# Moving the sample group's attention into the merge stage of a hybrid decoder step, with evacuations ranked first and a pipelined final stage

## Chip, cores, metric

One Trainium2 chip, all 8 cores (two dies of four). Each core runs the same program on one prompt sequence of 2048 tokens and on 16 of the 128 sample tokens. The metric is the device time of the slowest core, in microseconds. Runs come fast and slow (one die at a lower granted clock). Ratios are of fast runs. Medians are of all runs of a kernel; where one of these was slow (before, a_nosample, a_a2, the first session of the changed kernel), the median of its fast runs alone is at most 0.7 us lower.

## The reference, cut to what matters

```python
u = rmsnorm(x, norm_g); proj = u @ w_in                    # 1024 -> 8704 columns
lx, lg, sb, scg, sh, sg, q, qg, mg = split(proj)
xc = causal_dwconv(lx) + b; hs = rglru(xc)                 # A: gates, decay, scan over time
z_a = (hs * silu(lg)) @ lru_wo
z_b = (silu(sg) * sb * causal_dwconv(scg * sh)) @ sconv_wo # B
z_c = (softmax(q k / sqrt(128)) v * silu(qg)) @ xa_wo      # C: 256 memory tokens, 4 heads
g_a, g_b, g_c = split(sigmoid(mg))
y = x + (g_a*z_a + g_b*z_b + g_c*z_c) @ w_out              # then a final rmsnorm
```

The prompt group shares one set of keys and values per core. In the sample group each of the 16 tokens has its own 256 keys and values, so its attention is 16 small problems, each with a 512 KB key tile and a 512 KB value tile to fetch.

## The kernel before

The kernel is written as a graph of tasks with a rank (`prio`, smaller is earlier). At build time a planner with its own idea of durations fixes one order per engine; on the chip every engine follows its order strictly. So a changed rank is a changed order, and nothing on the chip corrects a bad one. Two words used below: a *unit* is the group of matmuls that fills one PSUM tile (16 for a projection), and its *evacuation* is the ScalarE or VectorE operation that reads that tile and so frees it for the next unit.

```python
PS = Ring("psum", ..., 4)                  # four PSUM tiles of 128 x 1024 fp32
def branch_A_lx(n, P):                     # one projection, three units of 688 columns
    for u, ps in enumerate(proj(C_LX + n * 128, P)):
        G.act(copy(lxp[u] <- ps), ..., P - 20 + u)         # evacuation: rank P - 20
    ...                                    # convolution on ScalarE and VectorE, rank P + 2
def branch_A_gates(n, P):                  # six gate units of 2 matmuls, tanh on ScalarE,
    ...                                    # then exp, exp, sqrt, multiply, scan
# planner: a task whose table set is not loaded counts as 20 later
for n in range(NCH + 1):                   # "block n": six channel blocks of 128
    branch_B_sb(n - 1); branch_A_gates(n); attend(n)       # attend only for n < 4
    branch_A_lg(n + 1)
    if n == 3:
        sample_scores(pos, 5.0)            # 16 x (broadcast matmul, multiply, reduce)
        sample_values(pos + 90, 1.5)       # 16 x 8 matmuls of one column
    branch_B_c(n - 1); branch_B_sg(n + 1); branch_A_lx(n + 1)
# merge stage: 8 column blocks, each: gate projection, tanh, output matmuls, multiply-add
# final stage: 17 row tiles
for ti in range(17):
    ps = mT @ wo                                            # 16 matmuls of 512 columns
    y = 0.5 * ps + x                                        # VectorE, line 1138
    stat = sum(y * y)                                       # ScalarE, line 1141
    rstd                                                    # GpSimd, lines 619, 621
    y = y * stat * fgb                                      # VectorE, line 1145
    store y   # writes t_dram[4], so each store waits for the last one
```

The softmax here doesn't subtract the row's maximum and nothing guards it: scores larger than these inputs give would overflow.

## Time and profile before

| what | value |
|---|---|
| first session, timed | 876.95 us median of 4 (873.47 to 881.83) |
| later session, timed | 859.72 us median of 8 (one of them slow) |
| profiled span, slowest core | 858.4 us |
| blocks (116.6 to 487.2 us) | 370.6 us, 82 more than TensorE's work takes at full pace |
| merge (487.2 to 771.2) | 284.0 us, TensorE busy 283.1 |
| final (771.2 to 858.4) | 87.2 us, against 58.8 of matmuls |

How to read it: TensorE does most of the work, so time is either TensorE's own or time in which it waits. The share of the chain that ended last says how much is left to win. Part 4 of the page gives that chain by engine:

```profile
PE 64%; ACT 9%; DVE 9%; issue 9%; DMA 4%; POOL 3%; ACTq 1%; DVEq 0%; POOLq 0%; SPq 0%
```

64% of the span lay on TensorE, and 36% on other engines, on transfers and on issue. For the final stage the view of waits on VectorE (what waited, what for: total us, times, longest) names the two reasons:

```profile
DVE R L1145 <- POOL R L621: 27.2, 13, 2.5
DVE R L1138 <- DMA y_p<-R: 6.5, 1, 6.5
```

VectorE stood 27.2 us for the norm from GpSimd (13 tiles, 2.5 us each at most), in order, so the next residual and with it the next PSUM tile waited too.

### The profile page before, as it was taken

The numbers are of one execution on the slowest core, as the hardware profiler recorded it, in microseconds if no ns is written. First come the engines' busy times: TensorE is split into PE (matmuls) and PEld (weight loads), VectorE is DVE, ScalarE is ACT, GpSimd is POOL, SyncE is SP. The second block draws the span as 40 slices with busy tenths as digits, with TensorE's granted clock in tenths as the row PEclk, the third lists the DMA queues.
The fourth block names the chain that finished last, engine by engine and source line by source line (L and its number), as shares of the span: only waits on it lengthen the run. The fifth ranks groups of instructions, "written<-read, shape, count | busy, mean of one in ns | idle before, by whom it ended". The sixth has DMA issues, their size and how long they took to land.

```text
span 858.4 us, 13185 instructions; the slowest of 8 cores (848.3 to 858.4 us)
## 1 busy us (share of the span) xinstructions
PE 742.9 (87%) x4859; PEld 460.8 (54%) x4859; DVE 386.3 (45%) x367; ACT 339.1 (40%) x398; POOL 251.2 (29%) x301
## 2 busy tenths in 40 slices
PE   0699989789888977979896699999999999999880
PEld 0466546356445544536554466666666666664330
DVE  0432244637636636798978161222222122224364
ACT  2355378784684484446354122112122221212221
POOL 2875200202002111101224234436344352232121
PEclk9999999889989989989998899999999999999996
DMA  6897962223223325556265559343443340019632
GB/s 133 215 181 108 147 98 26 24 26 38 25 39 36 37 26 87 119 122 135 44 85 70 74 62 125 32 40 35 40 42 38 34 40 2 1 26 316 237 136 101
DMA packets 109449, 68.67 MB, mean 80 GB/s; under 512 B 90819, under 2 KB 97045, under 8 KB 109371
## 3 DMA queue, kind: packets, MB, share of 16 engines
q0 software_dynamic: 96640, 30.81, 34.4%
q1 hardware_dynamic: 12508, 36.69, 13.3%
q8 instruction: 40, 0.66, 0.3%
q10 hardware_dynamic: 239, 0.34, 0.2%
q14 instruction: 22, 0.18, 0.1%
HBM read 88.96 MB, written 9.82 MB: 115 GB/s over the span
## 4 chain that ended last, share of the span: by engine, by line
PE 64%; ACT 9%; DVE 9%; issue 9%; DMA 4%; POOL 3%; ACTq 1%; DVEq 0%; POOLq 0%; SPq 0%
PE PP L726 61%; DVE R L804 2%; ACT R L1141 2%; DMA y_p<-R 2%; DVE R L1138 2%; ACT R L790 2%; DVE R L777 1%; POOL R L621 1%; DMA R<-sconv_w 1%; DVE R L803 1%; ACT R L939 1%; DMA R<-cv 1%; PE PP L866 1%; DVE R L838 1%; POOL R L633 1%
## 5 line engine op out<-in xcount | busy, mean ns | idle before, releaser
L726 PE MATMUL PP<-R 128*128 128x344 bf16 x4104 | 632.0, 315 | 34.4 <-ACT R L790 7.7
L726 PEld LDWEIGHTS PP<-R 128*128 128x128 bf16 x4104 | 402.1, 99 | 256.9 <-issue 55.4
L1101 DVE SCALAR_TENSOR_TENSOR R<-R,PP 128x688 f32<-128x688 f32 x72 | 62.7, 871 | 202.8 <-PE PP L726 202.7
L131 POOL DMA_DIRECT2D R<-w_in x68 | 60.4, 889 | 307.0 <-PE PP L726 270.3
L1095 ACT ACTIVATE R<-PP 128x688 f32<-128x688 f32 x72 | 53.6, 744 | 218.4 <-PE PP L726 218.4
L1134 PE MATMUL PP<-R 128*128 128x512 bf16 (+1 forms) x272 | 60.0, 379 | 8.4 <-DVE R L1138 7.3
L1105 POOL TENSOR_TENSOR R<-R 128x688 f32<-128x688 f32 x24 | 39.3, 1639 | 45.6 <-DVE R L1101 44.1
L1134 PEld LDWEIGHTS PP<-R 128*128 128x128 bf16 (+1 forms) x272 | 25.9, 97 | 42.3 <-issue 11.9
L1141 ACT ACTIVATE R<-R 128x1024 f32<-128x1024 f32 (+1 forms) x17 | 18.0, 1056 | 65.9 <-DVE R L1138 65.7
L1108 POOL TENSOR_TENSOR R<-R 128x688 bf16<-128x688 f32 x24 | 38.7, 1637 | 16.9 <-DVE R L1101 16.9
L777 DVE SCALAR_TENSOR_TENSOR R<-R 128x2048 f32<-128x2048 f32 x18 | 42.2, 2347 | 2.7 <-ACT R L774 1.9
L642 DVE TENSOR_TENSOR R<-PP,R 128x1024 bf16<-128x1024 bf16 (+1 forms) x19 | 22.1, 1175 | 43.6 <-PE PP L639 43.6
L1145 DVE SCALAR_TENSOR_TENSOR R<-R 128x1024 f32<-128x1024 f32 (+1 forms) x17 | 21.8, 1283 | 28.6 <-POOL R L621 27.2
L619 POOL TENSOR_SCALAR R<-R 128x1 f32<-128x1 f32 (+1 forms) x36 | 8.7, 242 | 87.8 <-ACT R L1141 63.3
L838 DVE SCALAR_TENSOR_TENSOR R<-R 128x2048 f32<-128x2048 f32 x12 | 28.2, 2348 | 8.8 <-ACT R L835 8.4
L790 ACT ACTIVATE R<-PP,R 128x688 f32<-128x688 f32 x36 | 28.1, 833 | 6.8 <-PE PP L726 6.7
L1138 DVE SCALAR_TENSOR_TENSOR R<-PP,R 128x1024 f32<-128x1024 f32 (+1 forms) x17 | 20.5, 1218 | 14.5 <-DMA y_p<-R 6.5
L804 DVE TENSOR_TENSOR_SCAN R<-R 128x2048 f32<-128x2048 f32 x6 | 26.5, 4422 | 0.4
L639 PE MATMUL PP<-R 128*128 128x128 bf16 (+1 forms) x152 | 14.0, 248 | 14.4 <-POOL R L633 13.0
L771 ACT COPY R<-PP 128x688 f32<-128x688 f32 x18 | 13.2, 732 | 29.9 <-PE PP L726 29.9
L829 ACT COPY R<-PP 128x688 f32<-128x688 f32 x18 | 13.0, 730 | 28.8 <-PE PP L726 26.1
L835 ACT ACTIVATE R<-R 128x2048 f32<-128x2048 f32 x6 | 12.0, 1999 | 30.9 <-DVE R L769 18.1
(121 smaller groups left out, 571.3 us busy)
## 6 DMA issues: line engine op xcount, KB each, us to landing
R<-w_in POOLq DMA_DIRECT2D x68, 256.0 KB, 4.6
R<-xp SPq DMA_DIRECT2D x32, 512.0 KB, 7.5
R<-ck SPq DMA_DIRECT2D x16, 512.0 KB, 4.3
y_p<-R SPq DMA_DIRECT2D x16, 512.0 KB, 2.7
R<-cv POOLq DMA_DIRECT2D x16, 256.0 KB, 7.4
R<-w_out POOLq DMA_DIRECT2D x8, 256.0 KB, 7.4
R<-lru_wo POOLq DMA_DIRECT2D x8, 192.0 KB, 3.9
R<-sconv_wo POOLq DMA_DIRECT2D x8, 192.0 KB, 4.1
```

Of the source, the lines that this page charges most:

```text
L131: eng.dma_start(out=out, in_=in_).then_inc(sems[semkey], 16)
L726: return lambda e: e.matmul(ps.ap[:, b * 512:b * 512 + BLK], lhs(k), rhs[:, k, c:c + BLK], start=(k == 0), stop=(k == nk - 1))
L777: G.dve(lambda e, k=k: e.scalar_tensor_tensor(out=xc[:, 0:T], in0=lxp[:, k:k + T], scalar=cw(k), in1=xc[:, 0:T], op0=ALU.mult, op1=ALU.add ...
L790: G.act(lambda e, ps=ps, dst=dst, u=u, bcol=bcol: e.activation(out=cols(dst, u), in_=pv(ps), func=AF.Tanh, scale=0.5, bias=dv[:, bcol:bcol ...
L804: G.dve(lambda e: e.tensor_tensor_scan(out=xc[:, 0:T], data0=thr[:, 0:T], data1=thi[:, 0:T], initial=0.0, op0=ALU.mult, op1=ALU.add), T, t ...
L838: G.dve(lambda e, k=k: e.scalar_tensor_tensor(out=cy[:, 0:T], in0=cinp[:, k:k + T], scalar=sw(k), in1=cy[:, 0:T], op0=ALU.mult, op1=ALU.ad ...
L1095: G.act(lambda e, ps=pg[u], th_=th_: e.activation(out=b3(th_.ap), in_=pv(ps), func=AF.Tanh, scale=0.5), UW, [pg[u].tok], [th_.tok], Px - 2 ...
L1101: G.dve(lambda e, zp=zp, th_=th_, dst=dst: e.scalar_tensor_tensor(out=b3(dst.ap), in0=b3(th_.ap), scalar=1.0, in1=pv(zp), op0=ALU.add, op1 ...
L1105: G.pool(lambda e, acc=acc, th_=th_: e.tensor_tensor(out=acc.ap, in0=acc.ap, in1=th_.ap, op=ALU.add), 1.6, [acc.tok, th_.tok], [acc.tok], Px)
L1108: G.pool(lambda e, acc=acc, th_=th_, u=u, j=j: e.tensor_tensor(out=mT[:, j, u * UW:(u + 1) * UW], in0=acc.ap, in1=th_.ap, op=ALU.add), 1.6 ...
L1134: return lambda e: e.matmul(ps.ap[0:nr, b * 512:(b + 1) * 512], mT[:, k, c0:c0 + nr], wo[:, k, b * 512:(b + 1) * 512], start=(k == 0), sto ...
L1138: G.dve(lambda e, ps=ps, y_=y_, x_=x_, nr=nr: e.scalar_tensor_tensor(out=y_.ap[0:nr, :], in0=ps.ap[0:nr, :], scalar=0.5, in1=x_.ap[0:nr, : ...
```

## The change

Intent: take the sample attention out of the blocks, where VectorE is short, and put it where VectorE idles; keep PSUM flowing by ranking evacuations first; let the final stage run at TensorE's pace.

```diff
+EV = 100
+AB = 20
-  [ps.tok], [t_lx[u]], P - 20 + u          # and so for every evacuation
+  [ps.tok], [t_lx[u]], P - EV + u
-  ... [t_xcP], P + 2)                      # branch A chain
+  ... [t_xcP], P + 2 - AB)
-  k += 20.0                                # table set not loaded
+  k += 40.0 if t.tset else 15.0            # 15: a matmul whose reader needs another set
-  m_a2 = Mem("a2", m_lxp.off, TT, F32)     # decay term over the convolution input
+  m_a2 = side("a2", 0, TT, F32)
-  NW = 12                                  # weight buffers; early loads get a second ring
+  NW = 10
 # sample attention: from block 3 to the merge, its buffers over those of w_out
-  if n == 3: sample_scores(pos, 5.0); sample_values(pos + 90, 1.5)
+  if j == 0: sample_scores(P, 5.0)
+  if j == 3: sample_values(P - 20, 1.0)
+  # column blocks 0 to 4 are merged before the sample columns are ready: keep their tanh and
+  # sum in thS, acS and redo those 16 columns after block 5
+  if j == NJS: fix_samples(P + 6)
 # final stage
-  for xi, x in enumerate((0, 1, 2)):
+  for xi, x in enumerate((0, 1, 2) if j < 7 else (2, 1, 0)):   # frees C's and B's memory early
+  x_ = Handle(xaring if ti % 10 < 4 else xgring)               # one ring for each
+  if last is not None: G.after(last, res)   # scale of tile t behind residual of t + 1
-  store(..., [y_.tok], [t_dram[4]])
+  store(..., [y_.tok], [])
... (cuts: the planner's durations, buffer offsets, one V ring rule)
```

## The prediction

> **What bounds the kernel now.** I read the profile in this order: the page's slices, a table of busy time by stretch that I cut at the first gate matmul of each of the six channel blocks, TensorE's waits, then the timeline at three places. The slices first; the last line is the clock granted to TensorE in tenths:
>
> ```profile
> PE   0699989789888977979896699999999999999880
> DVE  0432244637636636798978161222222122224364
> PEclk9999999889989989989998899999999999999996
> ```
>
> One slice is 858.4/40 = 21.5 us. From slice 23 to 36 TensorE is at 9 and at full clock: the merge stage, which no evacuation order can shorten. The losses lie before it (sevens, sixes and a lowered clock) and after it (eights). VectorE is at 7 to 9 in slices 16 to 20 only. The stretches:
>
> ```profile
> 167.40:233.60 66.20, 59.54 (x369) 36.13 (x370) 37.23 (x32) 42.12 (x45) 9.42 (x13) 0.93 0.29 29
> 233.60:301.90 68.30, 59.47 (x372) 36.12 (x373) 37.39 (x32) 43.05 (x46) 9.41 (x13) 0.95 0.30 35
> 301.90:379.30 77.40, 63.79 (x371) 36.33 (x371) 51.16 (x44) 39.47 (x41) 10.84 (x15) 0.91 0.47 79
> 379.30:441.50 62.20, 57.93 (x358) 34.78 (x359) 56.39 (x45) 31.41 (x29) 11.71 (x16) 0.95 0.49 93
> 441.50:487.20 45.70, 30.75 (x288) 19.58 (x287) 25.02 (x25) 20.09 (x20) 16.58 (x18) 0.85 0.66 92
> 487.20:771.20 284.00, 283.13 (x1947) 189.95 (x1944) 73.29 (x81) 54.56 (x72) 111.80 (x95) 1.00 0.36 39
> 771.20:858.40 87.20, 59.99 (x272) 25.87 (x272) 41.38 (x35) 19.53 (x34) 17.23 (x36) 0.90 0.56 197
> ```
>
> Columns: stretch, length, busy us (and count) of PE, PEld, DVE, ACT, POOL, then granted clock, DMA share, GB/s. The merge row gives a yardstick: 1936 matmuls of 344 columns by the program's order in 283 us, so 0.146 us each. A 512-column one costs 0.216 us (the final stage's 3.46 us for 16). By these, blocks 0 to 5 (116.6 to 487.2 us, 370.6 us long) hold 40.3, 55.1, 56.0, 57.8, 53.0 and 26.3 us of TensorE work: a full block is 348 matmuls x 0.146 = 50.8, plus its attention matmuls, plus 0.36 for each broadcast of the sample scores (6.5 us over 407 ns mean, with 16 of them). What is lost is 10.5, 11.1, 12.3, 19.6, 9.2 and 19.4 us: **82 us**. The two long ones hold the sample attention:
>
> ```profile
> PE PP L1003 <- DMA R<-cv: 13.7, 2, 6.9
> PE PP L726 <- ACT R L790: 7.7, 14, 1.4
> PE PP L964 <- DVE R L832: 4.8, 1, 4.8
> ```
>
> TensorE stood twice for 6.8 and 6.9 us for a value tile (buffers reused at once in a ring of two), and 4.8 us because VectorE was full. Each such pause costs again afterwards:
>
> ```profile
> 340.96 0.58 PE L964 MATMUL PP<-R 16*128 16x512 bf16 x1 [4.76 <-DVE R L832]
> 341.74 7.33 PE L726 MATMUL PP<-R 128*128 128x344 bf16 x32 [0.20 <-DVE R L832]
> 349.01 0.39 PE L964 MATMUL PP<-R 16*128 16x512 bf16 x1
> 349.33 4.84 PE L726 MATMUL PP<-R 128*128 128x344 bf16 x32
> ```
>
> The same 32 matmuls take 7.33 us after the pause and 4.84 us once warm: 2.5 us more.
>
> In the final stage, VectorE is the in-order engine that ties a loop:
>
> ```profile
> 813.10 3.61 PE L1134 MATMUL PP<-R 128*128 128x512 bf16 x16 [1.32 <-DVE R L1138]
> 814.75 0.55 POOL L621 TENSOR_TENSOR R<-R 128x1 f32<-128x1 f32 x1
> 815.47 1.28 DVE L1145 SCALAR_TENSOR_TENSOR R<-R 128x1024 f32<-128x1024 f32 x1 [2.52 <-POOL R L621]
> 816.67 2.35 DVE L1138 SCALAR_TENSOR_TENSOR R<-PP,R 128x1024 f32<-128x1024 f32 x2
> ```
>
> It adds the residual (L1138), idles 2.52 us while ScalarE and GpSimd make the norm, scales (L1145), and only then frees the next PSUM tile. So a tile costs 4.93 us (811.73 to 816.67) and TensorE needs 3.46. Earlier in that stage VectorE waits 6.5 us for a store, since each store waits for the last one, and the first stores run behind twelve 512 KB reloads issued at 770.4.
>
> **What the Trainium skill says.** "TensorE: Matmul & The Clock Gate", Part 1 (the HAM clock gate): after about 3.4 us of idleness the array runs at half clock until about 3.4 us of work have passed. The trace agrees: 7.33 against 4.84 us above, after 4.76 us. "Perfetto Trace Analysis", Optimization Strategy: where the contended engine changes with the regime, interleave the regimes. That is the move here: VectorE is 91% busy in block 4 (56.4 of 62.2 us) and 26% in the merge (73.3 of 284). "ScalarE: Activation LUTs", What ACT_TABLE_LOAD costs: about 1283 ns for the load. The trace shows 1283 ns each, 32 of them in the program. "DMA: Bandwidth & Descriptors", Issuing engines are not separate DMA queues: all transfers share 16 engines. The trace agrees in the first store, 15.8 us behind the reloads on the chain that ended last.
>
> **The change part by part.** I also compared the two programs' instruction orders, which the diff does not give.
>
> 1. *Sample attention goes to the merge.* Out of blocks 3 to 5 go 16 x (1.22 + 1.22) = 39 us of VectorE work, 16 key and most value loads, and 9.4 us of TensorE work (16 x 0.36, 128 small matmuls of 0.025, transposes). That TensorE work comes back in the merge, so it nets zero. The gain is the waits: 13.7 us for values and some 4 us of cold clock after them, and about 9 us of excess in block 3 over block 2.
>
> 2. *Evacuations first, chain of branch A 20 earlier, a buffer of its own for the decay term (before it lay over the convolution's input).* The build's order shows what this does: the gates of block n+1 used to come about five units after the last convolution input, and now come after six branch-B and six further units, some 28 us of TensorE work against the 11 us (scaling 2.1, three times 2.35, cast 1.9) that the convolution needs. ScalarE's order holds 32 table loads before and after, so nothing is saved there. What stays is the burst of six gate units (6 x 0.83 = 5 us of ScalarE for 1.75 us of matmuls) and attention (about 9 us of ScalarE for 5.2 us of matmuls). For 0 to 5 I estimate losses of 8, 7, 7, 7, 4 and 3 us, so 36 in place of 82. This is the softest step. Parts 1 and 2 together: **-46 us**.
>
> 3. *The merge pays.* Fix-up: 20 small matmuls, two tiny VectorE operations, ten small copies and tanhs, all beside TensorE work but for about 1 us. Scores: a key buffer turns round in 4.3 us landing plus 1.2 us of multiplying, so two give one per 2.8 us, against 16 scores spread over some 400 matmuls (59 us, 3.7 us apart). VectorE will stand for a key now and then, and with it the evacuations behind; the four PSUM tiles hide most. I put 4 us. Values: eight buffers for sixteen tiles. Four tiles are consumed, then two units (4.7 us) follow, and then a tile is wanted whose buffer has just come free and takes 7.4 us to land plus about 0.9 to issue: a wait of some 3.5 us, and another for the last four. With a little cold clock, 9 us. Sum **+14 us**, and 10 us of moved work besides.
>
> 4. *Final stage.* The scale of tile t is forced behind the residual of t+1, so VectorE needs 2.5 us a tile and the norm (2.9 us) hides in TensorE's 3.46. Stores no longer wait for one another. Ten reloads start when the last column block has read branch C and then B, some 12 to 25 us before the stage. So 17 x 3.46 = 58.8, plus 0.3, plus the last tile's tail, 7.7 us as now (850.7 to 858.4): 66.8 in place of 87.2, **-20 us**.
>
> Sum: -46 + 14 - 20 = -52, so a span of 806 us. The timed runs of before stand at 879.9 against a profiled span of 858.4, a ratio of 1.025 whose cause the profile doesn't tell; applied to 806 it gives **826**. I take 824.
>
> **Rivals.** *(a) TensorE is fed all through:* blocks then lose some 15 us and the merge almost nothing. Span about 775, timed 795. For it: ScalarE has only about 43 of 68 us to do in a block, VectorE 37. Against it: both are in order, a scan takes 4.4 us at a stretch and a burst of gates outruns ScalarE whatever the ranks. *(b) The waits move along:* the chain tanh, exponentials, root, scan still sets the block, as it did in blocks 1 and 2 where no sample work was, so only the excess of blocks 3 and 5 and the final stage are gained, and the merge loses 20 to key and value loads. Span about 835, timed 855. For it: block 2 lost 12 us with idle VectorE. Against it: that loss sits around the gates and attention, where the order did change. *(c) Reloads collide:* key and value loads of 16 MB run beside merge weights, at a DMA share of 0.36 now; if weights come late TensorE stands. I give this little, as weights are asked for far ahead.
>
> **Range and chances.** Rival (a) sets the low end, 794, rival (b) the high end, 850; the final stage's 20 us is in all of them and alone is 2.3%. Over 2% faster means under 862: 0.96; within 2% 0.035; slower 0.005.
>
> **What would show it.** Right: final stage about 67 us with a residual every 3.5 us, no wait of it for a store; blocks 2 and 3 alike at 60 to 63 us with VectorE under 40 busy; no value wait before the merge; merge near 308 us with waits for values and keys of some 10 us. Wrong: blocks still over 66 us with waits for gates and attention (rival b); a merge over 320 us; a final tile slower than 3.6 us.

## The result

The changed kernel took **789.42 us** (median of 4; 788.98, 789.36, 789.49 fast, 861.73 slow with die 0 at clocks of 0.886 to 0.919). The ratio was 0.901 [0.895, 0.907] in that session and **0.917 [0.915, 0.919]** in the later one, where before took 859.72 us and the changed kernel 788.56 us on the same chip. A ratio is the mean time of one kernel's fast runs over that of the other's of the same rounds, so it is not quite the ratio of the medians quoted. Of the two ratios 0.917 is the one to keep (see a_again: what slowed before in the first session is open). Either time is below the predicted range (794 to 850) and far from 824.

The chain that ended last, of the changed kernel:

```profile
PE 85%; issue 3%; DMA 3%; POOL 3%; ACT 3%; DVE 2%; ACTq 0%; POOLq 0%; DVEq 0%
```

85% in place of 64% lies on TensorE. The slices (span 787.1 us, so 19.7 us each) show where:

```profile
PE   0599998999999988999999989998999999999995
...
DVE  0432344356854953958684888621221221222675
...
PEclk9999998999999999999999999999999999999999
```

The clock row shows a single 8 (slice 7) where before had eights again and again. VectorE's solid band is broken into single peaks of 8 or 9; its one solid stretch left, three eights in slices 23 to 25 (433 to 492 us), is the scores, now in the merge, and TensorE stands at 9, 8 and 9 above it. The same by stretch, cut at the first gate matmul of each of blocks 0 to 5 and at the final stage (columns as in the prediction):

```profile
110.50:181.90 71.40, 65.83 (x390) 39.34 (x394) 31.12 (x29) 57.26 (x63) 9.05 (x11) 0.93 0.26 24
181.90:228.80 46.90, 45.52 (x307) 29.58 (x307) 34.77 (x28) 30.99 (x31) 8.47 (x12) 1.00 0.34 33
228.80:281.00 52.20, 49.67 (x325) 31.31 (x325) 36.28 (x29) 37.18 (x39) 10.51 (x12) 1.00 0.37 36
281.00:340.00 59.00, 54.56 (x355) 34.21 (x356) 36.71 (x33) 44.03 (x45) 10.87 (x13) 1.00 0.32 30
340.00:383.20 43.20, 42.08 (x287) 27.70 (x286) 31.56 (x23) 28.02 (x26) 8.44 (x12) 1.00 0.34 32
383.20:719.50 336.30, 328.49 (x2330) 215.97 (x2329) 139.31 (x143) 77.16 (x99) 139.48 (x130) 0.99 0.60 91
719.50:787.10 67.60, 58.48 (x266) 26.20 (x270) 42.03 (x35) 19.54 (x34) 15.13 (x36) 0.97 0.50 181
```

By the yardstick of the prediction (0.146 us a matmul of 344 columns, 0.216 of 512), and the units that the program's order puts between those marks (300, 300, 332 and 284 matmuls of 344; 4, 24, 24 and 0 of attention), blocks 1 to 4 hold 44.7, 49.0, 53.7 and 41.5 us of work. They lose 2.2, 3.2, 5.3 and 1.7 us, at a granted clock of 1.00. In before the blocks 1 to 4 lost 11.1, 12.3, 19.6 and 9.2 us at 0.91 to 0.95. Block 0 did not improve: its 348 matmuls of 344 and 44 of 512 are 60.3 us of work in 71.4, so it loses 11.1 us (10.5 before), at a clock of 0.93 and with ScalarE busy for 57.3 us. Its waits are the attention's, 1.8 us at most, and after two of them (1.7 and 1.3 us) 16 matmuls that took 2.50 us at 120.8 us take 4.59 us at 130.7. TensorE's longest waits that are left in blocks and merge:

```profile
PE PP L744 <- ACT R L808: 4.9, 12, 0.5
PE PP L1075 <- DMA R<-cv: 3.7, 5, 1.0
PE PP L942 <- DVE R L958: 3.4, 2, 1.8
PE PP L744 <- DVE R L1133: 1.9, 2, 1.1
```

The gate bursts (L808) wait 12 times and never over 0.5 us. The value tiles cost 3.7 us in five waits of at most 1.0 us, in place of 13.7 in two. In the final stage the timeline and VectorE's waits answer to what before showed at 813 us:

```profile
736.44 0.55 POOL L639 TENSOR_TENSOR R<-R 128x1 f32<-128x1 f32 x1
736.88 1.23 DVE L1176 SCALAR_TENSOR_TENSOR R<-PP,R 128x1024 f32<-128x1024 f32 x1 [1.04 <-PE PP L1172]
738.02 1.28 DVE L1185 SCALAR_TENSOR_TENSOR R<-R 128x1024 f32<-128x1024 f32 x1
740.33 1.23 DVE L1176 SCALAR_TENSOR_TENSOR R<-PP,R 128x1024 f32<-128x1024 f32 x1 [1.04 <-PE PP L1172]
```

```profile
DVE R L1176 <- PE PP L1172: 20.6, 17, 2.6
```

The residual of a tile (L1176) now comes every 3.45 us (736.88 to 740.33), the scale of the tile before (L1185) follows it without a wait, and VectorE waits for TensorE, not the other way round.

### The profile page after: what moved, and what is told of

It is laid out like the page before. It is cut to its first block, busy times and chain, and to the rows that moved or that the text cites. A ratio compares the mean times of both kernels' runs of the same rounds, so it can differ in the third digit from the quotient of the medians.

```text
span 787.1 us, 13219 instructions; the slowest of 8 cores (781.2 to 787.1 us)
## 1 busy us (share of the span) xinstructions
PE 727.2 (92%) x4864; PEld 460.0 (58%) x4879; DVE 388.1 (49%) x369; ACT 339.7 (43%) x403; POOL 257.1 (33%) x311
## 4 chain that ended last, share of the span: by engine, by line
PE 85%; issue 3%; DMA 3%; POOL 3%; ACT 3%; DVE 2%; ACTq 0%; POOLq 0%; DVEq 0%
PE PP L744 73%; PE PP L1172 7%; DMA R<-cv 2%; PE PP L950 1%; POOL R L651 1%; ACT R L808 1%; DMA R<-sconv_w 1%; PE PP L884 1%; PE PP L657 1%; POOL R L639 1%; DVE R L822 1%; PE PP L942 1%; PE PP L1036 1%; ACTq L133 0%; ACT R L945 0%
## 5 line engine op out<-in xcount | busy, mean ns | idle before, releaser
L744 PE MATMUL PP<-R 128*128 128x344 bf16 x4104 | 618.0, 311 | 9.9 <-ACT R L808 4.9
L744 PEld LDWEIGHTS PP<-R 128*128 128x128 bf16 x4104 | 400.0, 98 | 219.2 <-issue 22.1
L1124 ACT ACTIVATE R<-PP 128x688 f32<-128x688 f32 x72 | 53.5, 743 | 228.7 <-PE PP L744 223.7
L1133 DVE SCALAR_TENSOR_TENSOR R<-R,PP 128x688 f32<-128x688 f32 x72 | 62.6, 871 | 159.5 <-PE PP L744 151.6
L1176 DVE SCALAR_TENSOR_TENSOR R<-PP,R 128x1024 f32<-128x1024 f32 (+1 forms) x17 | 20.8, 1224 | 20.6 <-PE PP L1172 20.6
L808 ACT ACTIVATE R<-PP,R 128x688 f32<-128x688 f32 x36 | 27.7, 832 | 5.8 <-PE PP L744 5.5
L637 POOL TENSOR_SCALAR R<-R 128x1 f32<-128x1 f32 (+1 forms) x36 | 6.8, 188 | 67.5 <-ACT R L1181 44.5
L850 DVE TENSOR_TENSOR R<-PP,R 128x688 f32<-128x688 f32 x18 | 15.7, 874 | 21.8 <-PE PP L744 21.8
L958 DVE TENSOR_TENSOR R<-PP,R 128x512 f32<-128x512 f32 x16 | 10.9, 687 | 30.0 <-ACT R L956 22.0
L647 ACT ACTIVATE R<-R 128x1024 bf16<-128x1024 f32 (+1 forms) x19 | 20.0, 1055 | 9.6 <-DMA R<-xp 9.0
L816 DVE SCALAR_TENSOR_TENSOR R<-R 128x2064 f32<-128x2064 f32 x6 | 13.9, 2309 | 18.0 <-ACT R L808 18.0
```

Of the source, the lines that this page charges most:

```text
L744: return lambda e: e.matmul(ps.ap[:, b * 512:b * 512 + BLK], lhs(k), rhs[:, k, c:c + BLK], start=(k == 0), stop=(k == nk - 1))
L808: G.act(lambda e, ps=ps, dst=dst, u=u, bcol=bcol: e.activation(out=cols(dst, u), in_=pv(ps), func=AF.Tanh, scale=0.5, bias=dv[:, bcol:bcol ...
L1124: G.act(lambda e, ps=pg[u], th_=th_: e.activation(out=b3(th_.ap), in_=pv(ps), func=AF.Tanh, scale=0.5), UW, [pg[u].tok], [th_.tok], Px - E ...
L1133: G.dve(lambda e, zp=zp, th_=th_, dst=dst: e.scalar_tensor_tensor(out=b3(dst.ap), in0=b3(th_.ap), scalar=1.0, in1=pv(zp), op0=ALU.add, op1 ...
```

## Experiments

Kernels called "before with ..." start from the old kernel, the others from the new. Three kernels without sample attention give a wrong `y_sample`; everything else in them is right.

| run | median us | before in its rounds |
|---|---|---|
| b_final, b_rank | 838.13, 837.40 | 859.81 |
| a_nosample, a_oldrank | 767.94, 811.17 | 859.81 |
| a_again, a_a2 | 788.56, 789.42 | 859.72 |
| b_nosample, c_start | 819.41, 783.43 | 859.72 |
| b_both_nosample, a_ev20 | 773.40, 824.65 | 859.27 |
| a_ab0, a_chain | 789.47, 789.98 | 859.27 |

**b_final: the final stage alone.**

```diff
 before with
+  (2, 1, 0) for the last column block; xa and xg rings; six output buffers
+  G.after(last, res); store writes []
```

> The kernel before with the final stage of the change alone (scale of tile t held behind the residual of tile t+1, stores not chained, two reload rings, six output buffers, last column block in the order C, B, A). If step 4 of the prediction was right, the profiled span falls by about 20 us (858 to 838) and the final stage takes 66 to 68 us. If the final stage was only bound by the reloads and stores, a tile still takes 4.9 us and the gain is under 12 us.

Measured: 838.13 us, ratio 0.975 [0.973, 0.977], 21.7 us less. Step 4 of the prediction (20 us) holds. In its trace VectorE waits 20.6 us for TensorE in 17 waits and 1.3 us for the norm, once.

**b_rank: the ranks alone.**

```diff
 before with
+  EV = 100, AB = 20, penalties 40 / 15, the planner's new durations
```

> The kernel before with the ranks alone (evacuations by 100, branch A chain by 20, table-set penalties, the planner's durations), sample attention left in the blocks, decay term still over the convolution input, final stage old. Theory R (the order is what frees TensorE): the blocks give back most of their 82 us loss, span about 825 or less. Theory S (the sample work in the blocks is what stalls them): blocks 1 and 2 improve by some 5 us each at most, blocks 3 to 5 stay long, span 845 to 855.

Measured: 837.40 us, 22.4 us less. The stretches from the gates of block 1 to those of blocks 2, 3 and 4:

```profile
182.20:229.50 47.30, 45.92 (x310) 29.87 (x310) 34.74 (x28) 31.25 (x32) 12.69 (x12) 1.00 0.34 34
229.50:286.10 56.60, 52.57 (x341) 32.52 (x340) 37.08 (x31) 37.74 (x41) 11.53 (x12) 1.00 0.37 42
286.10:358.70 72.60, 55.69 (x330) 30.87 (x327) 50.44 (x42) 40.79 (x42) 10.83 (x15) 0.98 0.48 75
```

The span, 834.8 us, lies between the two theories' ranges, and each holds in its own blocks. By the same yardstick (300, 316 and 300 matmuls of 344; 4, 24 and 24 of attention; 8 broadcasts in the third) the three stretches lose 2.6, 5.3 and 20.7 us. Blocks 1 and 2, without sample work, are nearly as good as in the changed kernel (2.2 and 3.2). The stretch with the scores is 72.6 us against 59.0, with VectorE at 50.4 us against 36.7. So the ranks free blocks 1 and 2 and not the one with the scores. That VectorE's load is the reason is argued: TensorE's waits in that stretch are 10.7 us for ScalarE and 5.6 for VectorE.

**a_oldrank: the changed kernel with the old ranks.**

```diff
-EV = 100
-AB = 20
+EV = 20
+AB = 0
-  k += 40.0 if t.tset else 15.0
+  k += 20.0 if t.tset else 0.0
```

> The changed kernel with the old ranks (evacuations by 20, branch A chain by 0, penalty 20 for a set switch and none for matmuls), sample attention still in the merge, decay term in its own buffer, final stage new. Theory R: the blocks lose again what before lost in blocks 1 and 2 (11 to 12 us each), span about 825. Theory S: the blocks stay short, span within 10 us of 787.

Measured: 811.17 us, 22.6 us over the changed kernel (788.56). The span, 810.5 us, lies between the two theories again. So the ranks are worth 22 us with the sample work in the blocks and 22 us with it out (b_rank also took the planner's new durations, which this run kept): between these two parts there is no large interaction.

**a_nosample and b_nosample: no sample attention at all, new and old kernel.**

```diff
-  sample_scores(...); sample_values(...); fix_samples(...)
```

> The changed kernel without any sample attention (scores, values and fix-up left out; y_sample is wrong on purpose). It shows what the merge pays: 10 us of matmuls plus the waits. By my prediction (14 us of waits) the span would fall by about 24 us to 763; by the waits in the trace of the changed kernel (3.7 us for values, about 3.4 us for scores) it falls by about 17 us to 770.

> The kernel before without its sample attention (y_sample wrong on purpose). It gives the gross cost of that work in the blocks under the old ranks. By the prediction it is 27 us of waits and 9.4 us of matmuls: 859.8 to about 823 us. If the gain of moving it was undersized (the runs so far suggest 27 us net of a 21.5 us cost in the merge, so 48 gross), it comes to about 812 us. Without old-rank effects changing, block 4 falls from 62 to about 48 us.

Measured: 767.94 us and 819.41 us. The merge therefore pays 788.56 - 767.94 = 20.6 us for the sample work, against 24 predicted (14 of waits, 10 of work). In the old blocks the same work cost 859.72 - 819.41 = 40.3 us, against some 36 predicted. Moving it is worth about 20 us net.

**b_both_nosample: do the parts add up?**

```diff
 before with
+  the new ranks and the new final stage
-  sample_scores(...); sample_values(...)
```

> The kernel before with the new ranks and the new final stage, its old buffers, and without sample attention (y_sample wrong on purpose). The changed kernel without sample attention took 767.9 us. So far: the final stage gives 21.7 us alone, the ranks 22.4 us with the sample work in the blocks, and taking the sample work out of before 40.3 us, which sums to 84.4 and 775.4 us. If the ranks give more once VectorE is free of sample work (the parts feed each other), this run comes to about 768 us like the changed one. If the 8 us come from the new buffers and rings, it comes to about 775 us.

Measured: 773.40 us, 85.9 us under before; the sum of the three single gains is 84.4. They add up. The 5.5 us between this and the changed kernel without samples (767.94, on another chip) must come from what else differs: buffers and rings (weights, gates, exponentials, decay term). The two traces say where: in both, the same count of TensorE instructions lies before the gates of block 2 and before those of block 5. The same wait in the gates stands 0.6 us apart at block 2 (228.05 here, 228.61 in a_nosample) and 5.1 us the other way at block 5 (389.39 and 384.25). So the gain falls in blocks 2 to 4, not in the start, where the second ring for early weights works. Which of the other buffers makes it was not tested.

**a_a2: the decay term back over the convolution input.**

```diff
-  m_a2 = side("a2", 0, TT, F32)
+  m_a2 = Mem("a2", m_lxp.off, TT, F32)
```

> The changed kernel with the decay term again over the convolution input (one buffer), all else as changed. If the separate buffer matters (the next convolution input can't be evacuated before the decay term has been used), each of blocks 0 to 4 waits some 2 to 4 us there: 797 to 810 us. If the new order has moved that input late enough anyway, under 3 us of difference: 788 to 793 us.

Measured: 789.42 us against 788.56. The buffer of its own, which I had listed as part of the gain, does nothing here.

**a_ev20 and a_ab0: which rank?**

```diff
 a_ev20
-EV = 100
+EV = 20
 a_ab0
-AB = 20
+AB = 0
```

> The changed kernel with evacuations ranked by 20 as before, the branch A chain by 20 and the new set penalties kept. All three undone cost 22 us. If it is the evacuation rank that feeds TensorE, most of that comes back here: 803 to 811 us. If it is the grouping by table set and the earlier chain, under 6 us: 789 to 795 us.

> The changed kernel with the branch A chain not ranked earlier (0 in place of 20), evacuations at 100 and the new penalties kept. If the early chain matters, the gates find their input late in blocks 4 and 5, which have no attention to fill: 793 to 800 us. If the order holds without it, under 3 us: 788 to 792 us.

Measured: 824.65 us and 789.47 us. The early chain is worth nothing (0.9 us, within the noise). The evacuation rank is worth 36 us where the new penalty stands: outside both expected ranges, and more than the 22 us of all the ranks and penalties together. The reason is in ScalarE's order at block 2 of that run:

```profile
238.58 1.28 ACT L812 ACT_TABLE_LOAD   x1
239.88 2.11 ACT L812 ACTIVATE R<-R 128x2064 f32<-128x2064 f32 x1
242.08 2.11 ACT L814 ACTIVATE R<-R 128x2064 f32<-128x2064 f32 x1
244.10 1.91 ACT L945 ACTIVATE R<-PP 128x1024 bf16<-128x1024 f32 x2
...
245.24 2.59 PE L950 MATMUL PP<-R 128*128 128x512 bf16 x8 [2.48 <-ACT R L945]
```

The two long exponentials of the decay (L812, L814) go ahead of the attention's (L945), which hold PSUM tiles, and TensorE stands 2.48 us for them. Its wait for L945 sums to 20.2 us in that run. That the penalty of 40 is what lets the chain pass an evacuation ranked by only 20 is how the planner's code reads; the penalty alone was not run.

**a_chain: stores chained again.**

```diff
-  store(..., [y_.tok], [])
+  store(..., [y_.tok], [t_dram[4]])
```

> The changed kernel with each output store again behind the one before it, the held-back scale kept; VectorE's order is the same as in the changed kernel. If the pipelining on VectorE is what the final stage gained, this stays within 3 us of 789. If the chained stores bound it (a store lands in 2.7 us when alone, but the last reloads share the engines), the stage grows by 5 us or more and VectorE waits for stores.

Measured: 789.98 us, within 1.5 us of the changed kernel. The queue waits 24.5 us in 13 places for stores, and none of it reaches VectorE. What the final stage gained is, as the traces read, VectorE's order. A build (not a run) adds a caution: with the explicit link between scale and residual left out, the order on every engine is identical, so the line that looks like the pipelining does not make it in this version. With both left out, the link and the freed stores, a build puts several scales from tile 10 on back directly behind their own residuals. So each of the two stands in for the other; no run has both undone.

**a_again: both kernels on one chip.**

```diff
 (none: the changed kernel itself)
```

> The changed kernel itself once more, so that both kernels run on one chip in the same rounds. If the 876.95 us of before in the first session were a state of that session (here before gave 859.8 us in six of seven runs), the changed kernel stays at 789 to 791 us and the ratio to before is 0.918 to 0.920. If the timed runs of before are slower than its profiled run for a reason in the kernel, before comes to 875 or more again and the ratio to 0.90.

Measured: 788.56 us, and before 859.72 us in the same rounds, ratio 0.917. Before's 877 us belonged to that first session. Its timed runs have no record by core, so what slowed them is open; its profiled run of 860.31 us was already of the faster kind. All four timed runs are 1.9 to 2.9% above the fastest later one (857.29 us), so the ratio of 0.901 does not compare fast with fast.

**c_start: a version that beats both.**

```diff
-  G.act(exp of the lambda parameters, ...)             # first on ScalarE
+  first = G.act(exp of the lambda parameters, ...)
+  G.after(first, square of input tile 3)
+  G.after(first, evacuation of input tile 2)
+  squares read m_stat.t too                            # keeps the memset of stat ahead
```

> A try to beat both: the changed kernel with one reordering at the start. In it ScalarE's first instruction is an exponential of the parameters, which waits for the last of eight small parameter loads until 13.6 us, and the squares of the first input tiles stand behind it, though their tiles are likely there earlier. Here that exponential (and VectorE's three products of it) come after the first tiles. If the tiles are there by about 8 us, the first transposes start at about 13 us in place of 18.8 and the whole ends 4 to 6 us earlier, 784 to 786 us. If the tiles land late as well, or the rest of the start absorbs it, under 1.5 us.

Measured: 783.43 us (median of 6, 782.48 to 787.82), just under the expected 784 to 786 and 5.1 us under the changed kernel on the same chip; ratio to before 0.912 [0.910, 0.915]. The start of the changed kernel, then of this one:

```profile
13.57 1.28 ACT L717 ACT_TABLE_LOAD   x1 [13.57 <-DVE R L617]
18.80 1.01 PE L657 MATMUL PP<-R 128*128 128x128 bf16 x8 [5.67 <-POOL R L651]
```

```profile
4.90 1.28 ACT L647 ACT_TABLE_LOAD   x1 [4.90 <-DMA R<-xp]
13.01 2.72 PE L657 MATMUL PP<-R 128*128 128x128 bf16 x24
```

In this run ScalarE's first instruction was released by the first input tile at 4.90 us. In the changed kernel, whose loads are the same, ScalarE stood until 13.57 us for parameters that nobody needed yet. The transposes start at 13.0 in place of 18.8 us.

## Why the prediction was wrong

*Final stage: right.* Predicted 66.8 us; the stretch is 67.6, and alone it gave 21.7 us. But its reason was partly wrong: I credited the forced link and the freed stores, and neither matters while the other stands (a build, and a_chain).

*The merge's price: right in sum.* "Sum +14 us, and 10 us of moved work besides" makes 24; it is 20.6 (10 and the 7.1 us of waits named here make 17; the other 3.5 show in none of them). The scores' stalls are 3.4 us (L1133 and ScalarE's L1124 together) for 4 predicted. The values' are 3.7 us for 9 with cold clock: the waits came where I placed them, but each stayed at 1.0 us or less. Why they were so short no run here shows.

*The blocks: the mechanism was right, the size was not.* The step of the prediction that failed reads "For 0 to 5 I estimate losses of 8, 7, 7, 7, 4 and 3 us, so 36 in place of 82". For blocks 1 to 4 that is 25 us; measured are 12.4. (Block 0 erred the other way: 11.1 us for 8.) The term within it that was mis-sized most is the burst of gates, reckoned as 5 us of ScalarE against 1.75 us of matmuls, so about 3 us each. This is the burst of block 2 (both engines on one timeline):

```profile
229.08 4.53 ACT L808 ACTIVATE R<-PP,R 128x688 f32<-128x688 f32 x6 [1.37 <-PE PP L744]
...
230.05 0.45 PE L744 MATMUL PP<-R 128*128 128x344 bf16 x2 [0.49 <-ACT R L808]
...
230.78 0.45 PE L744 MATMUL PP<-R 128*128 128x344 bf16 x2 [0.27 <-ACT R L808]
...
231.58 0.45 PE L744 MATMUL PP<-R 128*128 128x344 bf16 x2 [0.35 <-ACT R L808]
...
232.52 0.38 PE L942 MATMUL PP<-R 128*128 128x512 bf16 x1 [0.49 <-ACT R L808]
```

ScalarE takes 4.53 us, as reckoned. TensorE waits 0.49, 0.27, 0.35 and 0.49 us, 1.6 in all: it had run three units ahead into free PSUM tiles, and it goes on to the next unit while ScalarE still holds the last ones. Over all six bursts the waits for L808 are 5.4 us, not 18: the 4.9 us of the gate matmuls (L744) shown above, and 0.5 us of the attention's matmuls (L942), also in the view of waits. No clock is lost with them: the stretches of blocks 1 to 4 stand at 1.00. The other term, attention (9 us of ScalarE against 5.2 of matmuls, so some 4 us in each of four blocks), came to 8.9 us of waits in all, 5.1 of them in block 0, where clock was lost as well.

*The scale: an argument without a cause.* "A ratio of 1.025 whose cause the profile doesn't tell; applied to 806 it gives 826." That step added 20 us. On the later chip before takes 859.72 us, with spans of 855.4 to 859.3 in its fast runs: there the ratio did not come back. Without the step the prediction would have been 806 to 808, still 18 too many, and the measured time would lie between the unscaled spans of its rivals (775 and 835).

So of the 37 us between 826 and 788.6, the scale made 20 (less the 1.5 us by which a time exceeds its span), and the sum of the parts, 806 against a span of 787.1, the remaining 19. Of these, blocks 1 to 4 gave 12.6, and block 5 with the merge about 7 (336.3 us with some 326 of work by the yardstick, so 10 lost in place of 3 and 14). Block 0 took 3 and the final stage 0.8 of it back. Some 4 us lie before the blocks, where the prediction saw no gain: the first gate comes at 110.5 us with 16 matmuls fewer before it, against 116.6. Rival (a), TensorE fed all through, was the nearest: span 775 predicted, 787 measured. Rival (b) is refuted by blocks 1 and 2, and rival (c) by a merge without waits for weights. Two slips in the prediction changed nothing: counted as it counts its slices, VectorE is at 7 and 8 in slices 9 and 21 too, and the 855 us of rival (b) lie outside the 850 that it is said to set.

Where the 71 us went, by runs: final stage 21.7, ranks 22, sample work 40.3 out of the blocks and 20.6 into the merge, and about 7 that no single run holds; b_both_nosample puts 5.5 of them on the other buffers.

## What to carry to other kernels

In a statically ordered kernel, try ranking whatever frees PSUM above the rules meant to save something else (a table load, a long chain). Here that one constant was worth 36 us beside the raised penalty, all ranks and penalties together 22, and the chain's own rank nothing. Move work from the stage where its engine is busiest to one where it idles, and price both ends: 40 us out and 21 in. Don't carry a ratio between two kinds of measurement into a prediction unless you know its cause.

## What the Trainium skill lacked or had wrong

- "ScalarE: Activation LUTs", What ACT_TABLE_LOAD costs, gives about 1283 ns plus about 1380 ns of drain for each switch of set. The load agrees; no drain shows in the trace of before, where all 32 loads are followed by an activation 1.29 or 1.30 us after their start. ScalarE's timeline there:

```profile
243.07 0.83 ACT L790 ACTIVATE R<-PP,R 128x688 f32<-128x688 f32 x1
243.91 1.28 ACT L939 ACT_TABLE_LOAD   x1
245.21 0.60 ACT L939 ACTIVATE R<-PP 128x512 f32<-128x512 f32 x1
```

The last tanh ends at 243.90 us, and the first activation under the new set starts at 245.21: 1.31 us for the whole switch.

- "TensorE: Matmul & The Clock Gate", Part 1, says that a die falls to 13/16 of the clock once three of its cores run dense matmuls, and that on the default power profile an all-core kernel's sustained matmuls should be planned at that rate (which profile this card has is not on record). Here all eight cores had a mean granted clock of 0.985 to 0.997 in fast runs, with TensorE 92% busy on the slowest. The slow run of this kernel had 0.886 to 0.919 on one die; what sets that state is not shown.
- No page has the order in which an in-order engine should serve PSUM evacuations, table switches and long chains; a_ev20 puts 36 us on it.
